# Two of four weight sums added by the vector engine in the second half's Strassen steps, and the down projection's first sums fetched one by one

## The chip, the cores and the metric

The kernel runs on one core of a Trainium2 chip. TensorE (PE in the profile) multiplies matrices, VectorE (DVE) and ScalarE (ACT) work element by element, GpSimd (POOL) and SyncE (SP) issue transfers here. Transfers run on sixteen DMA engines that all queues share. The metric is the device time of one execution in microseconds (us); the profile is one execution of its own, with its own time.

## The reference, cut to what matters

One layer of an encoder: a combined input projection, a recurrent group and an attention group, an output projection, and an MLP, for a sequence of 512 positions and a model width of 1024. The change lies in the MLP, whose hidden width is 4096:

```python
x = x + mix @ w_out[l]
h = rms_norm(x, mlp_norm_g[l])
x = x + jnp.square(jax.nn.relu(h @ w_up[l])) @ w_down[l]
return rms_norm(x, final_norm_g)
```

`w_up` is 1024 x 4096 and `w_down` 4096 x 1024, all in float32.

## The kernel before, in words

**Three products for one.** A float32 matrix is split into a high and a low part. `conv_hi` (line 236) rounds a raw weight tile to its high part `whi` on ScalarE, and `conv_lo` (line 244) subtracts that from the raw tile on VectorE and gives the low part `wlo`. `mm3` (lines 273 to 275) then multiplies high by high, one high by the other's low, and the reverse.

**Chunks.** All weights are cut into tiles of 128 x 1024 floats (512 KB), one chunk each, in the list `chunks`. While TensorE works on chunk c, `feed` converts chunk c + 3: the high part after the third, the low part after the fifth of its eight groups of products. There are four buffers each for `whi` and `wlo`. Chunks that come plainly from memory go through three buffers `wraw`; each `conv_lo` of such a chunk ends with `emit_dma` (line 223), which sends for the next plain chunk on SP's queue into the freed buffer.

**The MLP in two halves of 2048 hidden columns.** In each half some groups of four hidden tiles, called quads and named by their first tile f0, are done by Strassen's scheme (in Winograd's form) with seven block products instead of eight; single tiles are done plainly, and one of them stands in the middle of every quad:

```python
QKIND = ("11", "t1", None, "t2", "21", "t3", "22", "t4")
```

`None` is the plain tile. Kinds "11", "21", "22" use a block of the weights as it stands; t1 to t4 are sums of blocks: t1 = 12 + 11, t2 = t1 + 22, t4 = t2 + 21, t3 = 12 + 22. A Strassen step has 24 products of 256 columns, a plain tile 24 of 512. The first half has two quads; the second half runs tile 12, then the quads f0 = 0 with tile 13, f0 = 8 with tile 14, f0 = 4 with tile 15, and then its down projection.

**How a sum is made.** `load_t` fetches block 12 plainly on SP's queue (line 1144) and then lets an adding fetch on POOL's queue (line 1145) add block 11 (t1) or 22 (t3) to the tile in place. When t1's low part has been made, `conv_lo` sends an adding fetch of block 22 onto the same tile (line 250), which makes t2; after t2's low part another one of block 21, which makes t4. Each adding fetch waits on POOL's queue, in order, for the low part that last read the tile. The raw tiles of the sums have four buffers `tw`. `swap` exchanges the places of t2 and 21 in the order of conversion, not of use.

**Around a step.** `quad_evac` (lines 1153 to 1168) copies a step's result from the accumulators on ScalarE or adds it to an earlier one on VectorE, with the squared ReLU. When all four quarters of two hidden pairs are there, `up_pair` (lines 1076 to 1079) forms the sums of the activations for the down projection, and `next_a` splits finished ones into high and low parts (lines 1182 and 1187) in between.

**The down projection** is itself a Strassen scheme over four groups q = 0 to 3: chunks alternate (11, q) and (s1, q), then (s2, q) and (22, q), and so on. Its first sums s1 = 11 + 12 are made by `load_s1`, for each q a plain fetch on SP (line 1246) and an adding fetch on POOL (line 1247) into the tile `ts`, from which s2 and s4 follow by further adding fetches (line 255). In the second half all four are started in the quad f0 = 8:

```python
if half == 1 and unit[1] == 8:
    loads(4, late)
    late["t2", 7] = lambda: load_s1(1, ts)
```

`late[kind, k]` is called after group k of that step; `loads(f0, late)` starts t1's tile of quad f0 at the end of this quad's t1, and t3's at the end of 21.

**Order.** The instructions of TensorE, ScalarE, VectorE and GpSimd stand in the order of this code. SP's transfers are placed by a scheduler, as early as their buffers allow. Every queue works strictly in order.

Of the kernel before, what the change touches and what calls it, by code (L numbers as in the profile page):

```python
# [15 lines left out]
OP = mybir.AluOpType  # L16
# [19 lines left out]
NQ = HF // 4  # L36
# [54 lines left out]
def hybrid_kernel(ctx: ExitStack, tc, xw, xT, w_in, w_v, w_out, w_up, w_dn, gates, vecs, rel, onehot, fg, out):  # L91
    nc = tc.nc
# [21 lines left out]
    def f(t):  # L114
        return t.bitcast(FT)
# [67 lines left out]
    cu, cq, cd_ = {}, {}, []  # L183
# [19 lines left out]
    raws, splits = {}, {}  # L203
    st = {"rc": 0}

    def ublock(h, b, f):
        return w_up[h * HF + f + {"11": 0, "12": 1, "21": 2, "22": 3}[b]]

    def source(c):
        if not isinstance(c, tuple):  # L210
            return c
        return ublock(*c[:3]) if len(c) == 4 else wblock(*c)

    def wblock(h, b, q):
        return w_dn[h, int(b[1]) - 1, (int(b[0]) - 1) * NQ + q]
# [3 lines left out]
    def emit_dma():  # L219
        if plain:  # L220
            i = plain.popleft()
            r = stream.tile([P, 1024], FT, name="wraw", tag="wraw", bufs=3)
            nc.sync.dma_start(r, source(chunks[i]))
            raws[i] = r


    swap = {}
    for (h, f0, kind), i in cq.items():
        if kind in ("t2", "21"):
            swap[i] = cq[h, f0, {"t2": "21", "21": "t2"}[kind]]  # L230

    def conv_hi(i):
        if i < len(chunks):
# [5 lines left out]
    def conv_lo(i):  # L239
        if i < len(chunks):  # L240
            i = swap.get(i, i)
            r = raws.pop(i)
            lo = stream.tile([P, 1024], FR, name="wlo", tag="wlo", bufs=4)
            nc.vector.tensor_tensor(lo, r, f(splits[i][0]), op=OP.subtract)  # L244
            splits[i] += (lo,)
            c = chunks[i]
            if isinstance(c, tuple) and c[1][0] == "t":
                nxt = {"t1": ("t2", "22"), "t2": ("t4", "21")}.get(c[1])
                if nxt:
                    nc.gpsimd.dma_start(r, ublock(c[0], nxt[1], c[2]), accum_op=OP.add)  # L250
                    raws[cq[c[0], c[2], nxt[0]]] = r
            elif isinstance(c, tuple) and c[1][0] == "s":
                nxt = {"s1": ("s2", "22"), "s2": ("s4", "21")}.get(c[1])
                if nxt:
                    nc.gpsimd.dma_start(r, wblock(c[0], nxt[1], c[2]), accum_op=OP.add)
                    raws[cd_[c[0]] + {"s2": 2 * NQ + 2 * c[2], "s4": 6 * NQ + c[2]}[nxt[0]]] = r
            else:
                emit_dma()

    def feed(c, k):  # L260
        if k == 2:
            conv_hi(c + 3)
        elif k == 4:
            conv_lo(c + 3)

    def feed_q(c, k):
        if k == 1:
            conv_hi(c + 3)
        elif k == 5:
            conv_lo(c + 3)  # L270
# [331 lines left out]
    for i in (3, 4, 5):  # L602
        conv_lo(i)
# [43 lines left out]
    for n, (k, tt) in enumerate(steps):  # L647
        c = C_V + k // 2
# [12 lines left out]
        if n >= GA and n < GA + 12 and (n - GA) % 3:  # L661
            t, m = (n - GA) // 3, 2 * ((n - GA) % 3 - 1)
# [320 lines left out]
    c = C_WO + 4  # L983
# [158 lines left out]
    def load_t(half, n, f0):  # L1142
        t = work.tile([P, 1024], FT, name="tw", tag="tw", bufs=4)
        nc.sync.dma_start(t, ublock(half, "12", f0))
        nc.gpsimd.dma_start(t, ublock(half, {"t1": "11", "t3": "22"}[n], f0), accum_op=OP.add)
        raws[cq[half, f0, n]] = t

    def quad_evac(kind, f0, bank, keep):
# [91 lines left out]
        xf[tt] = g_("xf")  # L1240
        nc.vector.tensor_tensor(xf[tt], x1n[tt, 1], fgt[1], op=OP.mult)

    def load_s1(half, ts):
        for q in range(NQ):
            t = ts[:, q, :]
            nc.sync.dma_start(t, wblock(half, "11", q))
            nc.gpsimd.dma_start(t, wblock(half, "12", q), accum_op=OP.add)
            raws[cd_[half] + 2 * q + 1] = t
# [7 lines left out]
    ts = None  # L1256
    nr2 = {}
    for half in range(2):
# [6 lines left out]
        if half == 0:  # L1265
            start = 3
            load_t(0, "t1", 4)
            pu = [ps_("pu", "pj") for _ in range(start)]
            for k in range(KD):
                for i in range(start):  # L1270
                    mm3(pu[i], wk(c0 + i, k), h2k(k), k == 0, k == KD - 1)
                    if i == 0:
                        feed(c0, k)
                if k in (1, 2, 4, 5):
                    h_sums({1: 0, 2: 1, 4: 2, 5: 3}[k])
                if k == 3:
                    load_t(0, "t3", 4)
                if k == 3:
                    x1_transpose(0, 0)
                if k in (5, 7):  # L1280
                    h_hi("t1", k // 7)
                    h_lo("t1", k // 7)
            conv_hi(c0 + 4)
            conv_lo(c0 + 4)
            for i in (0, 1):
                up_evac(i, pu[i])
            conv_hi(c0 + 5)
            conv_lo(c0 + 5)
            up_evac(2, pu[2])
# [12 lines left out]
        def up_tile(ff, late=()):  # L1302
            p = ps_("pu", "pj")
            c = cu[half, ff]
            for k in range(KD):
                mm3(p, wk(c, k), h2k(k), k == 0, k == KD - 1)
                feed(c, k)
                if (ff, k) in late:
                    late[ff, k]()
                if k in (5, 7):  # L1310
                    next_a()
            up_evac(ff, p)

        def up_quad(f0, mid, late):
            bank, keep = {}, {}
            for kind in QKIND:
                if kind is None:
                    up_tile(mid, late)
                    continue
                x = {"t1": "c", "22": "c", "21": "b"}.get(kind, "a")  # L1320
                if x not in bank:
                    bank[x] = ps_("pu", {"a": "gs", "b": "pj", "c": "et"}[x])
                c = cq[half, f0, kind]
                hi, lo = splits[c]
                for n in range(8):
                    e, k = n // 4, n % 4
                    sl = slice(n * P, (n + 1) * P)
                    mm3(bank[x][:, e * TH:(e + 1) * TH], (hi[:, sl], lo[:, sl]), h_part(kind, k),
                        n == 0 and kind in ("11", "t1", "21"), n == 7, True)
                    feed(c, n)  # L1330
                    if (kind, n) in late:
                        late[kind, n]()
                    if n == 6:
                        next_a()
                quad_evac(kind, f0, bank, keep)

        def split_h(n, m):
            def run():
                h_hi(n, m)
                h_lo(n, m)  # L1340
            return run

        def xt(tt, n):
            return lambda: x1_transpose(tt, n)

        def loads(f0, late):
            late["t1", 7] = lambda: load_t(half, "t1", f0)
            late["21", 7] = lambda: load_t(half, "t3", f0)

        for unit in UNITS[half][start:]:  # L1350
            ready = set(opdone)
            late = {}
            if half == 0 and unit[1] == 4:
                late = {("11", 0): split_h("t2", 0), ("11", 5): split_h("t2", 1), ("t1", 1): split_h("t3", 0), ("t1", 6): split_h("t3", 1),
                        (3, 1): split_h("22", 0), (3, 6): split_h("22", 1),
                        ("t1", 5): xt(0, 1), ("t2", 5): xt(1, 0), ("21", 5): xt(1, 1), ("t3", 5): xt(2, 0), ("22", 5): xt(2, 1), ("t4", 5): xt(3, 0)}
                loads(8, late)
            if half == 0 and unit[1] == 8:
                late = {("11", 5): xt(3, 1), ("t1", 5): scale_neg, (12, 0): lambda: load_s1(0, ts)}
            if half == 1 and unit[1] == 12:  # L1360
                late = {(12, 1): split_h("t1", 0), (12, 5): split_h("t1", 1)}
            if half == 1 and unit[1] == 0:
                late = {("11", 1): split_h("t2", 0), ("11", 5): split_h("t2", 1), ("t1", 1): split_h("t3", 0), ("t1", 5): split_h("t3", 1),
                        (13, 1): split_h("22", 0), (13, 6): split_h("22", 1)}
                loads(8, late)
            if half == 1 and unit[1] == 8:
                loads(4, late)
                late["t2", 7] = lambda: load_s1(1, ts)
            if unit[0] == "q":
                up_quad(unit[1], unit[2], late)  # L1370
            else:
                up_tile(unit[1], late)
# [47 lines left out]
        for j in range(7 * NQ):  # L1420
            _, w, q = seq[j]
# [20 lines left out]
            if half == 0 and j == 25:  # L1442
                h_load()
                ts = big.tile([P, NQ, 1024], FT, name="ts", tag="bigA")
# [82 lines left out]
```

## Time and profile before

| What | Value |
|---|---|
| median of 3 runs | 556.71 us |
| lowest, highest | 556.18, 558.02 us |
| the profiled execution | 556.5 us |
| its span, first to last instruction | 554.7 us |
| granted TensorE clock | 0.998 |
| TensorE, weight load, VectorE, ScalarE, GpSimd busy | 98%, 82%, 76%, 61%, 13% |
| read from memory, written | 94.33 MB, 4.23 MB |

The page of the profile lists busy time by engine, then groups of instructions by line, operation and tile, written output <- inputs. The word after an arrow in a bracket or behind a bar is what ended the idle time before an instruction. Matmuls are pipelined, so their lengths overlap and a busy TensorE need not be at its peak; the distance between starts tells more. In the names, `pu` is an accumulator of the up projection and `pd` of the down projection, `h2h` and `h2l` the parts of the activations, `hh` and `hl` those of their Strassen sums, `whi` and `wlo` the parts of a weight chunk, `wraw`, `tw` and `ts` raw weights, `a` an activation tile, `as` a sum of such, `ah` and `al` parts of one.

### The profile page before, as it was taken

How to read it: one execution, taken by the hardware profiler on the slowest of the kernel's cores; microseconds unless marked ns; L12 is line 12 of the kernel's file. 1: busy time of each engine (PE TensorE's matmuls, PEld its weight loads, DVE VectorE, ACT ScalarE, POOL GpSimd, SP SyncE). 2: the span in 40 equal slices, each digit the busy share in tenths (PEclk: the TensorE clock that was granted, in tenths of full speed). 3: DMA queues.
4: the chain of work that ended last, by engine and by line, in shares of the span. 5: the costliest groups of instructions: out<-in, count | busy, mean ns of one | idle time of the engine just before them, and what ended most of it. 6: DMA issues, size and time to landing. Idle time of an engine off the chain costs nothing. (4 is left out here: it accounts for less than half of the span.)

```text
span 554.7 us, 7754 instructions
## 1 busy us (share of the span) xinstructions
PE 544.7 (98%) x2878; PEld 456.1 (82%) x2878; DVE 421.1 (76%) x614; ACT 335.7 (61%) x531; POOL 71.2 (13%) x93
## 2 busy tenths in 40 slices
PE   9999999999999999999999999999999989999994
PEld 7888888677768668899998888888899979888883
DVE  6897499987677538977659984976664768995894
ACT  7669993688776425577634553754543445655565
POOL 3480000000000010011110114010102200131000
PEclk9999999999999999999999999999999999999999
DMA  7814424454372226387895499997597974799804
GB/s 267 266 39 147 163 92 146 121 164 133 97 266 76 77 77 151 108 234 167 244 240 186 117 262 255 252 334 258 133 302 235 239 194 115 167 314 256 212 0 151
DMA packets 31028, 100.62 MB, mean 181 GB/s; under 512 B 3716, under 2 KB 4100, under 8 KB 30992
## 3 DMA queue, kind: packets, MB, share of 16 engines
q1 hardware_dynamic: 22560, 71.31, 36.6%
q0 software_dynamic: 7680, 27.71, 26.5%
q10 hardware_dynamic: 752, 1.12, 0.6%
q8 instruction: 22, 0.36, 0.3%
q14 instruction: 14, 0.11, 0.1%
HBM read 94.33 MB, written 4.23 MB: 178 GB/s over the span
## 5 line engine op out<-in xcount | busy, mean ns | idle before, releaser
L244 DVE TENSOR_TENSOR wlo<-wraw,whi 128x1024 fp32r<-128x1024 f32 x76 | 93.6, 1234 | 27.1 <-ACT whi L236 27.0
L236 ACT ACTIVATE whi<-wraw 128x1024 fp32r<-128x1024 f32 x76 | 80.3, 1057 | 37.6 <-PE pd L275 13.2
L273 PE MATMUL pd<-whi,ah 128*128 128x512 f32 x192 | 74.8, 390 | 0.1
L274 PE MATMUL pd<-wlo,ah 128*128 128x512 f32 x192 | 74.8, 390 | 0.0
L275 PE MATMUL pd<-whi,al 128*128 128x512 f32 x192 | 74.7, 389 | 0.0
L273 PE MATMUL pu<-h2h,whi 128*128 128x256 f32 (+1 forms) x216 | 71.9, 333 | 0.0
L274 PE MATMUL pu<-h2l,whi 128*128 128x256 f32 (+1 forms) x216 | 71.4, 330 | 0.0
L275 PE MATMUL pu<-h2h,wlo 128*128 128x256 f32 (+1 forms) x216 | 71.3, 330 | 0.0
L244 DVE TENSOR_TENSOR wlo<-tw,whi 128x1024 fp32r<-128x1024 f32 x28 | 34.3, 1223 | 24.1 <-ACT whi L236 24.0
L273 PE MATMUL pu<-hh,whi 128*128 128x256 f32 x160 | 45.7, 286 | 0.7 <-ACT whi L236 0.7
L275 PE MATMUL pu<-hh,wlo 128*128 128x256 f32 x160 | 45.4, 284 | 0.8 <-DVE wlo L244 0.8
L236 ACT ACTIVATE whi<-ts 128x1024 fp32r<-128x1024 f32 x24 | 25.5, 1062 | 32.7 <-PE pd L275 18.4
L274 PE MATMUL pu<-hl,whi 128*128 128x256 f32 x160 | 45.3, 283 | 0.0
L273 PEld LDWEIGHTS pu<-h2h,whi 128*128 128x128 f32 x216 | 41.0, 190 | 3.8 <-ACT x1n L1047 0.2
L275 PEld LDWEIGHTS pu<-h2h,wlo 128*128 128x128 f32 x216 | 41.0, 190 | 3.8
L274 PEld LDWEIGHTS pu<-h2l,whi 128*128 128x128 f32 x216 | 41.1, 190 | 3.6
L236 ACT ACTIVATE whi<-tw 128x1024 fp32r<-128x1024 f32 x28 | 29.5, 1053 | 23.1 <-DMA tw<-in_w_up_dram 13.3
L273 PEld LDWEIGHTS pd<-whi,ah 128*128 128x128 f32 x192 | 36.0, 188 | 8.0 <-issue 0.5
L274 PEld LDWEIGHTS pd<-wlo,ah 128*128 128x128 f32 x192 | 36.0, 188 | 7.6 <-DVE wlo L244 0.2
L275 PEld LDWEIGHTS pd<-whi,al 128*128 128x128 f32 x192 | 36.0, 188 | 7.4
L244 DVE TENSOR_TENSOR wlo<-ts,whi 128x1024 fp32r<-128x1024 f32 x24 | 29.3, 1221 | 16.1 <-ACT whi L236 16.0
L273 PEld LDWEIGHTS pu<-hh,whi 128*128 128x128 f32 x160 | 30.7, 192 | 1.3 <-ACT whi L236 1.2
(247 smaller groups left out, 1252.1 us busy)
## 6 DMA issues: line engine op xcount, KB each, us to landing
wraw<-in_w_up_dram SPq DMA_DIRECT2D x27, 512.0 KB, 4.3
ts<-in_w_dn_dram POOLq DMA_DIRECT2D x24, 512.0 KB, 13.0
wraw<-in_w_dn_dram SPq DMA_DIRECT2D x24, 512.0 KB, 7.9
tw<-in_w_up_dram POOLq DMA_DIRECT2D x20, 512.0 KB, 8.4
wraw<-in_w_in_dram SPq DMA_DIRECT2D x13, 512.0 KB, 3.4
tw<-in_w_up_dram SPq DMA_DIRECT2D x10, 512.0 KB, 9.3
wraw<-in_w_out_dram SPq DMA_DIRECT2D x8, 512.0 KB, 3.3
ts<-in_w_dn_dram SPq DMA_DIRECT2D x8, 512.0 KB, 10.4
```

Source lines behind the costliest of these rows:

```text
L236: act(hi, raws[i], AF.Copy)
L244: nc.vector.tensor_tensor(lo, r, f(splits[i][0]), op=OP.subtract)
L273: nc.tensor.matmul(o, lhsT=a[0], rhs=b[0], start=bool(first), stop=False, skip_group_check=on)
L274: nc.tensor.matmul(o, lhsT=a[0], rhs=b[1], start=False, stop=False, skip_group_check=on)
L275: nc.tensor.matmul(o, lhsT=a[1], rhs=b[0], start=False, stop=bool(last), skip_group_check=on)
```

## The change

Only the second half's quads change (`half` or `c[0]` equal to 1). The order of conversion in them becomes 11, t1, plain tile, 21, 22, t2, t3, t4; the order of use stays. 22's raw tile is added by VectorE onto t3's tile, which then holds block 12 alone, right after 22's low part is made; the adding fetch of 22 for t3 goes. 21's raw tile is held in its buffer, and after t2's low part VectorE adds it onto that tile, which makes t4; the adding fetch of 21 goes. The next plain fetch is sent after the add, so for 21 it is sent when t2 has been converted and not when 21 has. In the first half the new table gives the same order as before.

The down projection's first sums of the second half are started singly: q = 0 after the last group of t3 in the quad f0 = 8, and q = 1, 2, 3 in the quad f0 = 4, after the first group of 11, the first of t1 and the fifth of t2.

```diff
-    swap = {}
+    SPLIT = (("11", "t1", None, "21", "t2", "t3", "22", "t4"), ("11", "t1", None, "21", "22", "t2", "t3", "t4"))
+    swap, held = {}, {}
     for (h, f0, kind), i in cq.items():
-        if kind in ("t2", "21"):
-            swap[i] = cq[h, f0, {"t2": "21", "21": "t2"}[kind]]
+        if kind == "11":
+            for j in range(8):
+                if SPLIT[h][j] is not None:
+                    swap[i + j] = cq[h, f0, SPLIT[h][j]]
...
                 if nxt:
-                    nc.gpsimd.dma_start(r, ublock(c[0], nxt[1], c[2]), accum_op=OP.add)
+                    if c[0] == 1 and c[1] == "t2":
+                        nc.vector.tensor_tensor(r, r, held.pop("21"), op=OP.add)
+                        emit_dma()
+                    else:
+                        nc.gpsimd.dma_start(r, ublock(c[0], nxt[1], c[2]), accum_op=OP.add)
                     raws[cq[c[0], c[2], nxt[0]]] = r
+            elif isinstance(c, tuple) and len(c) == 4 and c[0] == 1 and c[1] == "21":
+                held["21"] = r
+            elif isinstance(c, tuple) and len(c) == 4 and c[0] == 1 and c[1] == "22":
+                t = raws[cq[c[0], c[2], "t3"]]
+                nc.vector.tensor_tensor(t, t, r, op=OP.add)
+                emit_dma()
...
         nc.sync.dma_start(t, ublock(half, "12", f0))
-        nc.gpsimd.dma_start(t, ublock(half, {"t1": "11", "t3": "22"}[n], f0), accum_op=OP.add)
+        if half == 0 or n == "t1":
+            nc.gpsimd.dma_start(t, ublock(half, {"t1": "11", "t3": "22"}[n], f0), accum_op=OP.add)
...
-    def load_s1(half, ts):
-        for q in range(NQ):
+    def load_s1(half, ts, qs=range(NQ)):
+        for q in qs:
...
             if half == 1 and unit[1] == 8:
                 loads(4, late)
-                late["t2", 7] = lambda: load_s1(1, ts)
+                late["t3", 7] = lambda: load_s1(1, ts, (0,))
+            if half == 1 and unit[1] == 4:
+                late = {(("11", 0), ("t1", 0), ("t2", 4))[q - 1]: lambda q=q: load_s1(1, ts, (q,)) for q in range(1, NQ)}
```

## The prediction

> **What bounds the kernel now.** I read the page's busy shares first, then busy time by stretches of the second half, then TensorE's instructions in order of time where a stretch is not full, then the chain that ends there, and last the queues that feed that chain.
>
> ```profile
> span 554.7 us, 7754 instructions
> PE 544.7 (98%) x2878; PEld 456.1 (82%) x2878; DVE 421.1 (76%) x614; ACT 335.7 (61%) x531; POOL 71.2 (13%) x93
> ...
> q1 hardware_dynamic: 22560, 71.31, 36.6%
> q0 software_dynamic: 7680, 27.71, 26.5%
> ```
>
> The second half of the MLP runs from 386.8 us. In the next fence the columns are the stretch, its length, and the busy time of each engine in it; the second stretch is the only one in which TensorE is not full before the end.
>
> ```profile
> core 0: us, PE busy (x) PEld busy (x) DVE busy (x) ACT busy (x) POOL busy (x), PEclk, DMA share, GB/s
> 386.80:454.40 67.60, 67.60 (x480) 63.87 (x479) 44.01 (x53) 29.34 (x41) 11.59 (x13) 1.00 0.87 232
> 454.40:457.10 2.70, 1.21 (x6) 0.58 (x6) 1.53 (x2) 2.62 (x4) 0.01 (x1) 1.00 0.04 15
> 471.20:547.90 76.70, 76.45 (x338) 62.76 (x336) 64.48 (x86) 47.91 (x72) 9.75 (x11) 1.00 0.70 185
> ```
>
> So a change that touches only feeding can win what lies in that one hole, and little more. The hole in TensorE's order of time (start, length, engine, line, operation):
>
> ```profile
> 454.23 0.39 PE L274 MATMUL pu<-h2l,whi 128*128 128x512 f32 x1
> 454.46 0.39 PE L275 MATMUL pu<-h2h,wlo 128*128 128x512 f32 x1
> 455.59 0.39 PE L273 MATMUL pu<-hh,whi 128*128 128x256 f32 x1 [0.74 <-ACT whi L236]
> 455.81 0.28 PE L274 MATMUL pu<-hl,whi 128*128 128x256 f32 x1
> 456.85 0.39 PE L275 MATMUL pu<-hh,wlo 128*128 128x256 f32 x1 [0.76 <-DVE wlo L244]
> 457.07 0.28 PE L273 MATMUL pu<-hh,whi 128*128 128x256 f32 x1
> 457.19 0.28 PE L274 MATMUL pu<-hl,whi 128*128 128x256 f32 x1
> ```
>
> Lengths overlap, so I count starts. A 512-column product starts 0.23 us after the one before it, a 256-column one 0.12. After 454.46 the next should start at 454.69 and starts at 455.59 (0.90 lost); then 0.22 for 0.12 (0.10), 1.04 for 0.12 (0.92), and 0.22 for 0.12 (0.10). The sum is **2.02 us**. It is the first product of step t2 in the last quad (f0 = 4), first its high and then its low weight part. The chain behind it (start, length, what):
>
> ```profile
> 440.75 13.65 DMA tw<-in_w_up_dram
> ...
> 454.48 1.07 ACT whi L236
> ```
>
> The DMA is the adding fetch that turns t1's tile into t2's, sent from POOL. Why it took 13.65 us shows on POOL's issues, and in what that line usually takes (least, median, most of ten):
>
> ```profile
> 426.08 0.88 POOL L250 DMA_DIRECT2D tw<-in_w_up_dram  x1 [10.07 <-DVE wlo L244]
> 426.62 1.23 POOL L1145 DMA_DIRECT2D tw<-in_w_up_dram  x1
> 427.17 4.29 POOL L1247 DMA_DIRECT2D ts<-in_w_dn_dram  x4
> 429.36 3.00 POOL L1145 DMA_DIRECT2D tw<-in_w_up_dram  x1
> 440.75 0.88 POOL L250 DMA_DIRECT2D tw<-in_w_up_dram  x1 [8.39 <-DVE wlo L244]
> ```
>
> ```profile
> DMA to landing us min/median/max: 5.2/5.5/13.6
> ```
>
> Seven adding fetches go out within 3.3 us, four of them the down projection's first sums. By the page's queue lines, 27.71 MB in pieces of 512 KB are 53 adding fetches, and 26.5% of 554.7 us shared among them is 2.8 us each on all sixteen engines; a plain fetch comes to 1.5 the same way. Seven at 2.8 are 20 us of work, to 446 without any plain fetch between them, so t2's, sent at 440.75, stands behind the last of them.
>
> **The change, part by part.**
>
> *Two adding fetches per quad go (t3's 22, t4's 21), in three quads.* Six times 2.8 is 17 us of DMA time out of the first stretch, where the DMA share is 0.87 of 67.6, or 59 us. TensorE is full there, so this is worth nothing by itself; it is a cause of the next item.
>
> *The four sums of the down projection are spread.* In the built program, POOL now has q0's sum behind t1's of the last quad, then t2's adding fetch (sent by the same low-part conversion as now, near 440.75), and only then q1, q2, q3. POOL does not follow TensorE: nothing but their landed first halves holds q1 to q3, so they go out directly behind t2's, which is ahead of them in the same queue. SP's plain fetches of those first halves stand early in SP's order (the first waits only for the reads of the saved activations), so POOL should not stand waiting for them. With the queue empty, t2's fetch should take the median, 5.5 us, and land at 446.3; at the 8.6 that a queue of a few would give, at 449.4. Its high part takes 1.07 us, so any landing before 453.5 is hidden. The DMA wait falls from 2.02 us to **0**. Below nothing it can't go, since TensorE has no other idle time there.
>
> *What is late next: DVE.* Conversions went 11, t1, tile, 21, t2, t3, 22, t4; they go 11, t1, tile, 21, 22, t2, t3, t4. t2's low part is one place later, and ahead of it stand 22's low part and the new add t3 += 22. DVE around the last quad:
>
> ```profile
> 440.78 0.69 DVE L1164 TENSOR_TENSOR a<-v,pu 128x512 f32<-128x512 f32 x1 [0.33 <-PE pu L275]
> ...
> 448.44 0.69 DVE L1079 SCALAR_TENSOR_TENSOR as<-as,a 128x512 f32<-128x512 f32 x1
> 449.04 1.22 DVE L244 TENSOR_TENSOR wlo<-wraw,whi 128x1024 fp32r<-128x1024 f32 x1
> 450.18 0.68 DVE L1187 TENSOR_TENSOR al<-a,ah 128x512 fp32r<-128x512 f32 x1
> 455.57 1.23 DVE L244 TENSOR_TENSOR wlo<-tw,whi 128x1024 fp32r<-128x1024 f32 x1 [4.71 <-ACT whi L236]
> ```
>
> From 440.78, released by TensorE, to 450.18 DVE has no idle time: evacuation and the pair sums of two finished pairs. Then it waits 4.71 us for t2's high part. Now that hole is filled. Back to back, a 1024-column operation holds DVE 1.14 us (449.04 to 450.18) and a 512-column one 0.60 (448.44 to 449.04). The new order from 449.04 is low part of 21, a split of 512, low part of 22, the add, a split, low part of t2: it starts at 449.04 + 1.14 + 0.60 + 1.14 + 1.14 + 0.60 = 453.66 and ends 1.23 later, at 454.89. TensorE wants it for the third product, at 454.69 + 0.24 = 454.93, and started 0.05 after the end in the profile (455.57 + 1.23 to 456.85). That is 0.01 late, so DVE is exactly on the edge. No row shows the add itself. The nearest two-input operations (mean length in ns after the bar):
>
> ```profile
> L244 DVE TENSOR_TENSOR wlo<-wraw,whi 128x1024 fp32r<-128x1024 f32 x12 | 14.6, 1221 | 4.2 <-ACT whi L236 4.2
> L1376 DVE SCALAR_TENSOR_TENSOR x1n<-pd,r,x1n 128x512 f32<-128x512 f32 x2 | 1.4, 744 | 0.0
> ```
>
> I take the first, the same width with both inputs in the same memory as here. The lower end is a t2 part in time, 0 lost. For the upper end I let every operation hold DVE for its full length: 1.22 + 0.68 + 1.22 + 1.22 + 0.68 + 1.23 = 6.25, ending at 455.29, 0.41 late, with 0.10 for the restart as above 0.5. An add like the second row, twice 0.744 or 1.49, makes it 0.8. I take **0.1**, since the spacing of starts is what these very operations show.
>
> Behind t2's low part stand the second add (t2 += 21), two splits, the tile's two squares and t3's low part: 454.80 + 1.14 + 4 x 0.60 + 1.23 = 459.6, wanted at 454.69 + 2 steps of 2.88 + 0.24 = 460.7. t3's and t4's high parts on ACT now wait for these adds (ready near 453.1 and 456.0) instead of adding fetches, ahead of the evacuations on ACT, and are wanted later than that; cost **0**, with 1.1 us to spare.
>
> *The other two quads.* A quad is seven steps of 24 products at 0.12 and a tile of 24 at 0.227, together 25.6 us, so t2's steps of the three quads start near 403.5, 429.1 and 454.7. DVE in the first one (f0 = 0):
>
> ```profile
> 394.58 1.23 DVE L244 TENSOR_TENSOR wlo<-wraw,whi 128x1024 fp32r<-128x1024 f32 x1 [0.25 <-ACT whi L236]
> 395.72 1.42 DVE L1133 TENSOR_TENSOR hl<-hs,hh 128x512 fp32r<-128x512 f32 x2
> 397.40 1.23 DVE L244 TENSOR_TENSOR wlo<-tw,whi 128x1024 fp32r<-128x1024 f32 x1 [0.26 <-ACT whi L236]
> 398.54 1.48 DVE L1133 TENSOR_TENSOR hl<-hs,hh 128x512 fp32r<-128x512 f32 x2
> ```
>
> At 397.40 would stand 22's low part, the add to 399.7, the two activation splits to 401.2, t2's low part to 402.5, wanted after 403.7: cost **0**. The second quad has neither splits nor pair sums there, so more.
>
> *Plain stream.* 21's block keeps one of three raw buffers until t2's low part is made, so the blocks behind it on SP are sent a tile later; they are wanted five and more steps on. 22's block is sent as now, but converted one step and one tile, 8.3 us, earlier. The tightest is that of the second quad, sent at 412 and so long on its way (line, size, us to landing; stretch 411.9 to 412.1):
>
> ```profile
> wraw<-in_w_up_dram SPq DMA_DIRECT2D x1, 512.0 KB, 11.7
> ```
>
> After its landing follow its high part (1.07), its low part and the add (1.14 each) and t2's low part (1.23), 4.6 us, in that order on ACT and DVE; t2's is wanted at 429.3. So it may land as late as 424.7, 12.7 us after it was sent; 11.7 would do, and that stretch loses two adding fetches. Cost **0**, by a cover of 1 us; without it, us for us.
>
> *The late sums.* q1 to q3 land at 2.8 us each behind 446.3, by 455; the first conversion that reads one of them comes after the last quad, near 469. Cost **0**.
>
> *Sum.* 2.02 - 0.1 = 1.9 us, with ends 1.2 (slow add) and 2.0. Against the profiled execution: 556.5 - 1.9 = 554.6. Its span is 554.7, with 1.8 around it; the median of the runs is 556.71, 0.2 above, so I give **554.8 us**, which is 0.34% less. What a measurement of this kernel can tell from no change is about 0.3%, or 1.7 us, so the forecast lies just past the edge.
>
> **Rivals.**
>
> *DVE takes part of it back.* Place: t2's low part in the last quad. Every 0.1 us that DVE is behind the row of starts above costs 0.1. With operations that never overlap, 0.5 is lost and the time is 556.7 - 1.5 = 555.2; with slow adds 555.5. For it: DVE has no slack left from 440.78 on. Against: starts 1.14 apart for 1.22 long. [...]
>
> *The gain is given back in the down projection, or t2 stays late.* ACT waited there once for a sum:
>
> ```profile
> ACT whi L236 <- DMA ts<-in_w_dn_dram: 6.0, 1, 6.0
> ```
>
> If the fetches there go at their own pace, TensorE comes 2 us earlier and waits 2 us: 556.7. Against: they are sent when buffers come free, so they move with TensorE, and TensorE is busy 76.45 of 76.70 us. The same time comes out if q0's sum holds POOL and t2's fetch is sent as late as 449.
>
> *Slower: the raw stream starves.* 22's fetch in the second quad takes longer than 12.7 us. Each us beyond is lost to TensorE; from 14.6 on the loss passes the gain of 1.9, and at 18 us 5.3 are lost and the time is 560.1. For it: 11.7 was seen, and there ACT's wait would hold everything behind it. Against: the fetch stood behind plain fetches of all four first halves, which SP's new order partly puts after it, and behind two adding fetches that are gone (5.6 us).
>
> **How the numbers follow.** Forecast 0.60; DVE takes part 0.16; given back 0.12; slower 0.12. The forecast's own spread, 554.2 to 555.2, crosses 555.04 (0.3%), so a little of it counts as no change: faster 0.53, same 0.35, slower 0.12. Range: from 554.0 (hole gone, and the 0.25 us of the down projection with part of the 0.2 between runs) to 557.2 (given back, with 0.5 for the spread of runs), leaving out the slower case.
>
> **What would show it.** Right: t2's adding fetch in the last quad 5 to 9 us long; three sums behind it; six new operations of 1.2 us on DVE; the step from the last tile's product to t2's first 0.23 us, and the low part at most 0.3 late; seven adding fetches from the line that is L250 now, and seven from L1145, instead of ten each. Wrong: ACT waiting for a raw block in the second quad past 424.7; a hole of TensorE in another quad or in the down projection; an add well over 1.3 us.

## The result, and the profile after

The changed kernel takes 553.73 us (median of 6 runs, 553.33 to 554.95); the kernel before, on the same chip, takes 556.68 (6 runs). The ratio is 0.9948, with a 95% interval from 0.9933 to 0.9963: faster, by 2.1 to 3.7 us. Forecast were 554.8 us and a range from 554.0 up; the time lies 0.27 us below that range. The profiled execution took 553.66 us. (Of two experiments below, e8 and e12, the profiled execution was disturbed; their traces are not read and their times leave it out.) The head of the page after:

```profile
span 551.9 us, 7746 instructions
PE 543.2 (98%) x2878; PEld 455.7 (83%) x2878; DVE 428.2 (78%) x620; ACT 336.0 (61%) x531; POOL 66.2 (12%) x87
...
q1 hardware_dynamic: 22560, 71.31, 37.0%
q0 software_dynamic: 6816, 24.57, 23.9%
```

Six adding fetches of 512 KB (27.71 - 24.57 = 3.14 MB) have gone from the software queue, and DVE has six operations more, for 7.1 us more. TensorE's work is the same. Busy time by stretches, the same ones as before, moved to where they now lie:

```profile
core 0: us, PE busy (x) PEld busy (x) DVE busy (x) ACT busy (x) POOL busy (x), PEclk, DMA share, GB/s
386.10:453.60 67.50, 67.50 (x480) 63.74 (x479) 51.99 (x61) 33.41 (x47) 8.03 (x9) 1.00 0.73 193
453.60:456.30 2.70, 2.70 (x22) 2.58 (x21) 2.67 (x4) 1.61 (x3) 0.00 (x0) 1.00 0.66 220
468.50:545.10 76.60, 76.35 (x338) 62.90 (x336) 63.37 (x84) 47.97 (x72) 9.78 (x11) 1.00 0.70 184
```

The stretch that had TensorE busy for 1.21 of 2.70 us is full. In the first one DVE rises from 44.01 to 51.99 us, and the DMA share falls from 0.87 to 0.73. TensorE in order of time, at the last quad's t2:

```profile
453.79 0.39 PE L288 MATMUL pu<-h2h,wlo 128*128 128x512 f32 x1
454.02 0.28 PE L286 MATMUL pu<-hh,whi 128*128 128x256 f32 x1
454.13 0.28 PE L287 MATMUL pu<-hl,whi 128*128 128x256 f32 x1
454.25 0.39 PE L288 MATMUL pu<-hh,wlo 128*128 128x256 f32 x1
454.47 0.28 PE L286 MATMUL pu<-hh,whi 128*128 128x256 f32 x1
```

t2's first product comes 0.23 us after the plain tile's last one, and the low part's product at its place; only the start behind that is 0.22 later instead of 0.12. Of the 2.02 us, 0.10 is left. The reason stands on POOL's queue (line 257 is the adding fetch of line 250 before, line 1261 that of 1247) and, in the second fence, in the landing times of all fetches of line 257:

```profile
440.07 0.87 POOL L257 DMA_DIRECT2D tw<-in_w_up_dram  x1 [22.94 <-DVE wlo L247]
440.62 3.03 POOL L1261 DMA_DIRECT2D ts<-in_w_dn_dram  x3
```

```profile
DMA to landing us min/median/max: 5.3/5.4/7.8
```

t2's fetch goes out at the old time, ahead of three of the sums, and takes 5.4 us instead of 13.65. POOL worked in order there: the first halves of those sums had been sent by 412.2 and took 7.5 us at most (line 1260), and the sums still went out behind t2's fetch, for which POOL waited 22.94 us. DVE there:

```profile
448.37 1.22 DVE L247 TENSOR_TENSOR wlo<-wraw,whi 128x1024 fp32r<-128x1024 f32 x1
449.50 0.69 DVE L1201 TENSOR_TENSOR al<-a,ah 128x512 fp32r<-128x512 f32 x1
450.10 1.22 DVE L247 TENSOR_TENSOR wlo<-wraw,whi 128x1024 fp32r<-128x1024 f32 x1
451.24 1.22 DVE L263 TENSOR_TENSOR tw<-tw,wraw 128x1024 f32<-128x1024 f32 x1
452.38 0.69 DVE L1201 TENSOR_TENSOR tw<-as,tw 128x512 fp32r<-128x512 f32 x1
452.98 1.22 DVE L247 TENSOR_TENSOR wlo<-tw,whi 128x1024 fp32r<-128x1024 f32 x1
454.23 1.23 DVE L254 TENSOR_TENSOR tw<-tw,wraw 128x1024 f32<-128x1024 f32 x1
```

This is the worked-out order, operation by operation, with no idle time in it. The low part ends at 454.20 and its product starts at 454.25.

By the starts of the first products of each stage (us; the last two columns are the second half):

| kernel, execution | second half starts | up projection | down projection |
|---|---|---|---|
| before, profiled | 386.79 | 84.37 | 76.10 |
| after, profiled | 386.12 | 82.38 | 75.96 |

The up projection lost 1.99 us, the down projection 0.14. The remaining 0.67 of the 2.82 us between the spans lies ahead of the second half: 0.32 ahead of the MLP and 0.35 in the first half's down projection (76.51 us before, 76.16 after). Up to there the two programs differ in one transfer alone: the adding fetch for t3 of the first quad, which goes out at 368.59 in the kernel before, is gone.

### The profile page after: what moved, and what is told of

The parts are those of the page before. It is cut to its first block, busy times and chain, and to the rows that moved or that the text cites. A ratio compares the mean times of both kernels' runs of the same rounds, so it can differ in the third digit from the quotient of the medians.

```text
span 551.9 us, 7746 instructions
## 1 busy us (share of the span) xinstructions
PE 543.2 (98%) x2878; PEld 455.7 (83%) x2878; DVE 428.2 (78%) x620; ACT 336.0 (61%) x531; POOL 66.2 (12%) x87
## 3 DMA queue, kind: packets, MB, share of 16 engines
q0 software_dynamic: 6816, 24.57, 23.9%
## 4 chain that ended last, share of the span: by engine, by line
PE 94%; DVE 2%; ACT 1%; DMA 1%; issue 0%; SPq 0%; ACTq 0%; DVEq 0%
PE pu L286 10%; PE pu L288 10%; PE pu L287 10%; PE pd L288 8%; PE pd L286 8%; PE pd L287 8%; PE pqk L286 3%; PE pwo L286 3%; PE pwo L288 3%; PE pqk L288 3%; PE pwo L287 3%; PE pqk L287 3%; PE pav L819 3%; PE pt L786 3%; PE pv L288 1%; PE pv L286 1%
## 5 line engine op out<-in xcount | busy, mean ns | idle before, releaser
L287 PEld LDWEIGHTS pu<-hl,whi 128*128 128x128 f32 x160 | 30.7, 192 | 0.2
```

The lines of the kernel that those rows point to most:

```text
L287: nc.tensor.matmul(o, lhsT=a[0], rhs=b[1], start=False, stop=False, skip_group_check=on)
```

## The experiments

Ratios are to the kernel before, run on the same chip beside each group.

**Chance and cause: both kernels once more, and each part of the change alone.** e1 is the kernel before and e2 the changed one, unchanged. e3 has only the sums spread (`load_s1` takes its new argument as in the change, here and in e6):

```diff
-                late["t2", 7] = lambda: load_s1(1, ts)
+                late["t3", 7] = lambda: load_s1(1, ts, (0,))
+            if half == 1 and unit[1] == 4:
+                late = {(("11", 0), ("t1", 0), ("t2", 4))[q - 1]: lambda q=q: load_s1(1, ts, (q,)) for q in range(1, NQ)}
```

e4 is the changed kernel with these lines put back, so that it has only the two adds on DVE.

> The kernel before, unchanged. The changed kernel gained 2.95 us by the medians and 2.8 by the two profiled spans, where the hole in front of t2 explains 2.0. In the profiles, 0.7 us of the rest lies ahead of the change: 0.3 in the first 30 us and 0.35 in the first half's down projection, where both programs are the same. Theory: that 0.7 is chance of single executions, and the hole itself differs between executions. Then the start of the second half (386.8 in the profile before, 386.1 after) falls anywhere from 386.0 to 387.5 here, and the hole anywhere from 1.5 to 3.5 us. Rival: the changed program's first part is really faster; then the second half starts at 386.8 +- 0.1 again, and the hole is 2.0 +- 0.1.

> The changed kernel, unchanged. Theory (chance ahead of the change): the second half starts between 386.0 and 387.5, the two after it (up projection and down projection) take 82.3 and 76.0 us as in the first profile, and the ratio to before is 0.995 to 0.997. Rival (the first part is really faster): the second half starts at 386.1 +- 0.1 again, and the ratio is 0.995 or less.

> The kernel before with the down projection's first sums started one by one as in the change; the adding fetches for t3 and t4 and the old order of conversion stay. Theory: the queue on POOL is all that made t2 late, and four sums were most of it; without them ahead t2's fetch takes 5 to 9 us instead of 13.6, its low part is made at once since the old order puts it before 22's, and the up projection takes 82.3 us as in the changed kernel: the whole gain, 2.0 us in the second half, ratio 0.995 to 0.997. Rival: the six adding fetches that went are needed too, because the queue is full without the sums; then t2 still lands past 453 and at least 0.7 us of the hole stays.

> The changed kernel with all four first sums started where they were before, after t2 in the quad f0 = 8; VectorE's adds and the new order stay. Theory: with two adding fetches per quad gone, the six that go out together from about 414 are worked off by 435, t2's fetch finds the queue empty and takes 5 to 6 us, and this part alone also gives the whole 2.0 us, ratio 0.995 to 0.997. So each part would do alone what both do together. Rival: the sums still hold up t2; then its fetch takes over 9 us and part of the hole is back.

| run | median us | ratio (95%) | second half starts | up | down |
|---|---|---|---|---|---|
| e1, before | 556.09 | 1.0002 (0.9989 to 1.0014) | 385.90 | 84.26 | 76.43 |
| e2, after | 553.57 | 0.9956 (0.9941 to 0.9970) | 385.79 | 82.39 | 75.96 |
| e3, sums spread | 554.09 | 0.9959 (0.9946 to 0.9973) | 385.56 | 82.29 | 75.97 |
| e4, adds only | 553.78 | 0.9954 (0.9940 to 0.9968) | 385.31 | 82.39 | 75.96 |

No gain shows in the first part of the kernel: e1 starts its second half 0.9 us earlier than the profiled execution of the same program. Both starts, 385.90 and 385.79, lie a little below the 386.0 that was the least expected. By the starts e1 loses 1.96 us at its hole, against 2.02. And either half of the change gives the whole gain. The adding fetches of line 250 (257 in e4) landed after (least, median, most) in e3 and in e4:

```profile
DMA to landing us min/median/max: 5.2/5.4/8.4
```

```profile
DMA to landing us min/median/max: 5.1/5.3/8.5
```

t2's own took 5.3 us in both. In e3 it overtakes the sums; in e4 they go out together as before, but the queue has fewer fetches and they have landed by 438.7, before t2's is sent. e3 has no hole at all, e4 the 0.10 that DVE leaves.

**How much one fetch ahead costs.** e6 is the kernel before with the last sum alone moved behind t2's fetch; e7 is the kernel before with 512 KB more of adding fetches behind the four sums, onto tiles that nothing reads.

```diff
-                late["t2", 7] = lambda: load_s1(1, ts)
+                late["t2", 7] = lambda: load_s1(1, ts, (0, 1, 2))
+            if half == 1 and unit[1] == 4:
+                late = {("t2", 4): lambda: load_s1(1, ts, (3,))}
```

```diff
-                late["t2", 7] = lambda: load_s1(1, ts)
+                def more():
+                    load_s1(1, ts)
+                    for i in range(2):
+                        t = g_("extra")
+                        nc.vector.memset(t, 0.0)
+                        nc.gpsimd.dma_start(t, w_dn[0, 0, 0, :, i * S:(i + 1) * S], accum_op=OP.add)
+                late["t2", 7] = more
```

> The kernel before, with three of the four sums of the down projection left where they are and only the last one sent behind t2's adding fetch of the last quad. Theory of the queue (each adding fetch ahead costs t2's about 3 us): t2's fetch lands 2.8 to 3.4 us earlier, near 451 us where up to 453.5 is hidden, so the hole of 2.0 us goes whole, the up projection of the second half takes 82.3 us, ratio 0.995 to 0.997. Rival, the gain goes by the number of sums moved: a quarter of it, 0.5 us, ratio 0.999, up projection 83.9.

> The kernel before, with 512 KB more of adding fetches (two of 256 KB onto tiles that nothing reads) sent directly behind the four sums, ahead of t2's of the last quad. Theory of the queue: t2's fetch lands 2.8 to 3.4 us later, the hole grows from 2.0 to 4.8 to 5.4 us, the kernel is about 3 us slower, ratio 1.005 to 1.006. Rival, the fetch was long for another reason (its own source rows, the plain fetches beside it): under 1 us more, ratio under 1.002.

e6 took 554.02 us, ratio 0.9963 (0.9950 to 0.9977); e7 560.76, ratio 1.0087 (1.0066 to 1.0107). t2's fetch in e6 (its issue, its landing time):

```profile
440.52 0.88 POOL L250 DMA_DIRECT2D tw<-in_w_up_dram  x1 [9.01 <-DVE wlo L244]
```

```profile
DMA to landing us min/median/max: 10.3/10.3/10.3
```

10.3 us instead of 13.65: 3.4 earlier for one fetch fewer, and this hides it whole (up projection 82.29). The chain in e7, and TensorE at the hole:

```profile
439.64 17.16 DMA tw<-in_w_up_dram
...
456.88 1.06 ACT whi L236
```

```profile
453.35 0.39 PE L275 MATMUL pu<-h2h,wlo 128*128 128x512 f32 x1
457.99 0.58 PE L273 MATMUL pu<-hh,whi 128*128 128x256 f32 x1 [4.25 <-ACT whi L236]
458.37 0.41 PE L274 MATMUL pu<-hl,whi 128*128 128x256 f32 x1
459.25 0.58 PE L275 MATMUL pu<-hh,wlo 128*128 128x256 f32 x1 [0.46 <-DVE wlo L244]
```

17.2 us: 3.5 more for one fetch more. So the length of t2's fetch went with the number of fetches ahead, by 3.4 and 3.5 us for one, and with one fewer TensorE saw nothing of it. The expected 3 us of time were too few, though: the up projection takes 89.35, 5.0 us more. The first starts behind the hole stand 0.38 us apart instead of 0.12; the clock, below, is why.

**Is DVE on the edge?** e5 is the changed kernel with t2's low part in the last quad computed three times over, e12 with it computed twice (the repeats change no value):

```diff
             lo = stream.tile([P, 1024], FR, name="wlo", tag="wlo", bufs=4)
+            if chunks[i] == (1, "t2", 4, "u"):
+                for _ in range(2):
+                    nc.vector.tensor_tensor(lo, r, f(splits[i][0]), op=OP.subtract)
             nc.vector.tensor_tensor(lo, r, f(splits[i][0]), op=OP.subtract)
```

> The changed kernel, with the low part of t2 in the last quad computed three times over instead of once (the two extra operations change no value). Theory that DVE stands exactly on the edge there: the finished low part comes 2 x 1.14 = 2.3 us later, TensorE waits 2.3 to 2.4 us ahead of its third product of t2 instead of 0.10, the up projection of the second half goes from 82.4 to 84.7 us, and the kernel is 2.3 us slower than the changed one, ratio to before 0.999 to 1.000. Rival, DVE has slack there or hands the delay on to work that nobody waits for: under 0.5 us more, ratio 0.995. Second question: if the small holes in the down projection of the second half (0.4 us before, none after) come from what a hole in the up projection leaves behind, they come back here and that stage takes 76.2 to 76.5 us; if the adding fetches caused them, it stays at 75.96.

> The changed kernel, with the low part of t2 in the last quad computed twice instead of once. Theory, DVE on the edge and the clock falling only after long holes: a hole of 1.14 + 0.10 = 1.24 us and no lower clock behind it, up projection 83.5 to 83.6 us, 1.14 to 1.3 us above the changed kernel, ratio to before 0.997 to 0.998, no run with a mean clock below 0.996. Rival, any hole lowers the clock: products 0.21 us apart for some 3 us behind it, 2.5 us above the changed kernel.

e12 took 554.99 us, ratio 0.9977 (0.9965 to 0.9989), 1.3 to 1.4 us above the changed kernel (553.57 in e2, 553.73), close to what no slack at all gives; its hole isn't shown. e5 took 557.63, ratio 1.0021 (1.0005 to 1.0036): slower than expected by more than a microsecond. DVE in e5:

```profile
453.06 2.48 DVE L249 TENSOR_TENSOR wlo<-tw,whi 128x1024 fp32r<-128x1024 f32 x2
455.57 1.23 DVE L250 TENSOR_TENSOR wlo<-tw,whi 128x1024 fp32r<-128x1024 f32 x1
456.83 1.23 DVE L257 TENSOR_TENSOR tw<-tw,wraw 128x1024 f32<-128x1024 f32 x1
```

The low part ends at 456.80, 2.60 us after that of the changed kernel; the repeats write one tile and start 1.25 apart, not 1.14. TensorE:

```profile
454.21 0.28 PE L290 MATMUL pu<-hl,whi 128*128 128x256 f32 x1
456.86 0.39 PE L291 MATMUL pu<-hh,wlo 128*128 128x256 f32 x1 [2.36 <-DVE wlo L250]
...
457.56 0.28 PE L290 MATMUL pu<-hl,whi 128*128 128x256 f32 x1
457.68 0.38 PE L291 MATMUL pu<-hh,wlo 128*128 128x256 f32 x1
457.85 0.41 PE L289 MATMUL pu<-hh,whi 128*128 128x256 f32 x1
458.06 0.41 PE L290 MATMUL pu<-hl,whi 128*128 128x256 f32 x1
```

The hole is 2.65 less the usual 0.12, or 2.53 us, as it should be. But 0.9 us behind it the starts go from 0.12 to 0.21 apart. The granted clock in stretches (the third number from the end):

```profile
core 0: us, PE busy (x) PEld busy (x) DVE busy (x) ACT busy (x) POOL busy (x), PEclk, DMA share, GB/s
456.60:457.80 1.20, 0.94 (x7) 0.95 (x8) 1.17 (x2) 0.00 (x0) 0.00 (x0) 0.97 0.00 0
457.80:460.90 3.10, 3.10 (x17) 3.10 (x16) 3.10 (x6) 0.00 (x0) 0.00 (x0) 0.50 0.56 166
460.90:463.00 2.10, 2.10 (x18) 2.10 (x18) 0.84 (x2) 1.54 (x2) 0.00 (x0) 0.95 0.01 4
```

After this hole of 2.53 us TensorE runs at a granted clock of 0.50 for the 3.10 us of the second stretch and for parts of its neighbours (0.97 and 0.95). Some 16 products that take 0.093 us more each are 1.5 us, which is most of the 1.7 us that e5 is later than expected (557.63 less 553.6 is 4.0, where 2.3 were worked out); the rest is the hole itself, 2.53 instead of 2.3. The second question of e5 got its answer too: its down projection takes 75.96 us, so the small holes there (0.08 us in the profiled execution before, 0.37 in e1) don't come from a hole in the up projection.

**Does the order on DVE alone decide?** e8 is e5 with t2 converted ahead of 22; e9 is the same kernel again, for its trace.

```diff
-    SPLIT = (("11", "t1", None, "21", "t2", "t3", "22", "t4"), ("11", "t1", None, "21", "22", "t2", "t3", "t4"))
+    SPLIT = (("11", "t1", None, "21", "t2", "t3", "22", "t4"), ("11", "t1", None, "21", "t2", "22", "t3", "t4"))
```

> As the run with the low part computed three times over, but with t2 converted ahead of 22 in the second half, so that 22's low part and the add t3 += 22 (together 2.28 us of DVE) stand behind t2's low part instead of ahead of it. Theory that only the order on DVE sets the end there: the extra 2.28 us are covered at t2 (hole there 0.1 as in the changed kernel), and t3's low part, which had about 1.0 us to spare, comes 2.28 us later, so TensorE waits 1.0 to 1.3 us at t3; up projection 83.4 to 83.7 us, time between the changed kernel and the run with the low part three times over, ratio about 0.997 to 0.998. Rival, t3 has more spare than worked out: no hole, ratio 0.995. Rival, something beside DVE holds t2: 2.3 us lost again, ratio 0.999 to 1.000.

> The run with t2 converted ahead of 22 once more, for its trace: its 555.3 to 555.6 us are 1.8 us above the changed kernel. Theory that only the order on DVE moved the wait: at t2 0.1 us are lost, at t3 1.0 to 1.3 us, two steps later, and the up projection takes 83.4 to 83.7 us; what is over of the 1.8 us then lies elsewhere. Rival: t2 waits still.

e8 took 555.34 us, ratio 0.9987 (0.9976 to 0.9999), e9 555.47, ratio 0.9994 (0.9978 to 1.0010); 0.997 to 0.998 were expected. In e9 nothing is lost at t2, and this two steps on:

```profile
459.90 0.27 PE L290 MATMUL pu<-hl,whi 128*128 128x256 f32 x1
461.57 0.39 PE L291 MATMUL pu<-hh,wlo 128*128 128x256 f32 x1 [1.41 <-DVE wlo L250]
461.80 0.28 PE L289 MATMUL pu<-hh,whi 128*128 128x256 f32 x1
```

With 0.10 for the restart 1.65 us are lost at t3's low part, where 1.0 to 1.3 were expected; the up projection takes 83.94 us. So the wait moved from t2 to t3 with the order, and of the 2.5 us that the two repeats take, t3 had about 1.0 to spare (2.5 less the 1.56 without a product). Behind this hole of 1.56 us the starts stay 0.12 apart.

**Does the hole of the kernel before lower the clock too?** e10 is the kernel before, unchanged. e11 is the kernel before with twelve products of zeros in the hole, so that TensorE idles less while t2's weights come no sooner:

```diff
+                if (half, f0, kind) == (1, 4, "t1"):
+                    zero[0] = g_("zero", FR)[:, :TH]
+                    nc.vector.tensor_scalar(zero[0], h2h[:, 0, left], 0.0, None, op0=OP.mult)
+                if (half, f0, kind) == (1, 4, "t2"):
+                    for n in range(12):
+                        nc.tensor.matmul(bank[x][:, 0:TH], lhsT=h2h[:, n % 8, left][:, 0:P], rhs=zero[0], start=False, stop=False, skip_group_check=True)
                 for n in range(8):
```

> The kernel before, unchanged, for the granted clock. With the low part computed three times over, the hole of 2.5 us at t2 was followed by 3.1 us at a granted clock of 0.50, which cost 1.4 us more than the hole. New theory: the hole of 2.02 us of the kernel before sets this off too, but only in some executions, since it is cut in two; those have a mean clock of 0.994 to 0.995 and a span near 555.2 us, the others 0.996 to 0.998 and near 554.0. Expected: about a quarter of the runs of the first kind, ten or more us apart from nothing else; if the profiled one is of it, the products behind t2's hole stand 0.21 us apart instead of 0.12 for about 3 us. Rival, the low mean clock comes from the start of the kernel, which varies by 1.2 us: then runs without the hole show it as often.

> The kernel before, with twelve products of a tile of zeros (256 columns, 0.12 us each, 1.44 us in all) added ahead of t2's first product in the last quad; they add nothing to the sums. t2's weights come no sooner, so the end of the hole stays where it is (low part at about 456.8), but TensorE idles there for 0.5 to 0.7 us instead of 2.02. Theory that idle time in the hole lowers the clock in some executions: no run has a mean clock of 0.995 or less, and the median is 0.2 to 0.4 us below that of before, ratio 0.9993 to 0.9996, near 554.0 us of span. Rival, the clock has nothing to do with the hole: as many low clocks as before, ratio 1.000; if the products delay t2 instead, 0.1 to 0.5 us more.

e10 took 556.46 us, ratio 1.0007 (0.9991 to 1.0022). Its profiled execution was one of those with a low mean clock (0.995, span 556.3). In stretches:

```profile
core 0: us, PE busy (x) PEld busy (x) DVE busy (x) ACT busy (x) POOL busy (x), PEclk, DMA share, GB/s
458.20:458.40 0.20, 0.20 (x4) 0.20 (x4) 0.20 (x1) 0.20 (x2) 0.11 (x1) 1.00 0.00 0
458.40:458.60 0.20, 0.20 (x4) 0.20 (x3) 0.20 (x1) 0.20 (x1) 0.00 (x0) 0.77 0.00 0
458.60:461.00 2.40, 2.40 (x13) 2.40 (x12) 2.40 (x5) 1.77 (x4) 0.00 (x0) 0.50 0.86 125
...
461.80:462.00 0.20, 0.20 (x3) 0.20 (x2) 0.20 (x1) 0.07 (x1) 0.00 (x0) 0.70 1.05 205
462.00:462.20 0.20, 0.20 (x4) 0.20 (x3) 0.20 (x1) 0.00 (x0) 0.00 (x0) 1.00 0.22 41
```

Its hole was the usual one (by the starts, 0.94 + 0.10 + 0.92 + 0.10 = 2.06 us), and 1.3 us after the low part's product at 457.20 the clock goes to half, from about 458.5 to 461.9, by the shares of the stretches at 0.77 and 0.70. The up projection takes 85.84 us, 1.5 more than in the other two profiles of this kernel. That is the direct sight of it; the runs give how often. In e7 the clock falls inside the hole, at 455.91 (0.80 over 453.30:457.70, then 0.50 to 462.60), and is back only 6.83 us later, which is where its time beyond the hole went. A mean clock of 0.995 or less over the whole execution (the hole is the time without a product by the starts, without the 0.10 behind each piece):

| kernels | hole, us | runs with it |
|---|---|---|
| before (in all groups with a clock for each run) | 1.8 in two pieces | 21 of 95 |
| after, e2, e3, e4, e6 | none | 1 of 30 |
| e12 | 1.25 (worked out) | 0 of 9 |
| e8, e9 | 1.56 | 0 of 17 |
| e5 | 2.53 | 8 of 10 |
| e7 | 4.4 and 0.8 | 4 of 4 |

Of the 95, those 21 have a mean span of 555.42 us, the others 554.20, so 1.2 us each. The start of the kernel can't be the reason: the kernels without the hole start in the same way, and only one of their 30 runs has the low clock, with a span (552.2) no longer than the others'.

e11 took 556.36 us, ratio 1.0005 (0.9993 to 1.0017). None of its 12 runs has the low clock, which at 21 in 95 has a chance of 5%. Its median isn't lower, though, as expected by 0.2 to 0.4 us; the interval reaches from 0.4 us of gain to 0.9 of loss, so this side is not settled. The products cost a little themselves: they end too late for t2's first product, and its low part comes 0.1 us later than in the profiled execution before (up projection 84.45):

```profile
454.26 1.59 PE L1332 MATMUL pu<-zero,h2h 128*128 128x256 f32 x12
455.69 0.28 PE L273 MATMUL pu<-hh,whi 128*128 128x256 f32 x1
455.81 0.28 PE L274 MATMUL pu<-hl,whi 128*128 128x256 f32 x1
456.55 0.39 PE L275 MATMUL pu<-hh,wlo 128*128 128x256 f32 x1 [0.46 <-DVE wlo L244]
```

## Why the prediction was right, and where it was wrong

**The hole and its cause: right.** t2's fetch stood behind other adding fetches, and was expected to take 5.5 us with the queue empty; it took 5.4. The price of 2.8 us for each fetch ahead was low: e6 and e7 measure 3.4 and 3.5 on either side. It changed nothing: the 10.3 us of e6 already left no hole, and t2's fetch took 5.4.

**DVE on the edge: right.** The worked sum said 0.01 late and 0.1 lost; 0.10 was lost. The add that no row of before showed took 1.22 us, the row it was taken from, and starts stand 1.14 apart. With that the rival in which operations don't overlap, with 555.2 us, falls: the rows from 450.10 to 452.38 start 1.14 us apart for 1.22 of length. Where an operation writes the tile that the one before it reads or writes, the rows here show no early start: in e5 the repeats start 1.25 us apart for 1.23 of length, and the add behind t2's low part starts 1.25 after it (452.98 to 454.23). e12 and e5 show the edge from the other side: each operation more ahead of t2's low part is paid in full. The 1.1 us to spare at t3 held: in the changed kernel its low part is done at 459.00 and its product starts at 460.10, and in e9 2.5 us of delay left TensorE 1.56 without a product.

**The other costs of nothing: right.** No hole appeared in another quad. 22's block of the second quad, for whose landing I had about 1 us of cover, kept nobody waiting: ACT converted it at 420.74 straight after the evacuation before it. The down projection took nothing back, since 75.96 us is the least of all traces. So the given-back and the slower rival fall too. The 17 us of DMA time taken out of the first stretch were too many: of the six adding fetches one went out ahead of it (368.59) and one behind it (457.1), and its DMA share fell from 0.87 of 67.6 to 0.73 of 67.5, or by 9.5 us. TensorE was full there, so nothing hung on it.

**The sum's base, and the low end of the range: wrong.** The step was "against the profiled execution: 556.5 - 1.9 = 554.6", with 0.2 to the median of the runs, and the end of 554.0 that allowed the 0.25 us of the down projection and part of 0.2 between runs. Against all runs the 554.8 were 1.1 us too high. The base is 0.6 of this: 556.71 was the median of three runs, and that of the 95 runs of the kernel before in the table above is 556.10. The gain is the other 0.5: down to 553.69, the median of twelve runs of the changed kernel, it is 2.4 us, where 1.9 were forecast. Three things were mis-sized.

First, the spread from one execution to the next in the shared part. The second half started at 386.79 in the profiled execution, and between 385.56 and 387.10 in the seven traces of kernels that are the same up to there (385.31 to 386.20 in the five with one adding fetch fewer). That alone can be the 0.67 of the 2.82 us between the two profiles. I took 0.2 from two times that happened to lie close together.

Second, the clock. I priced the hole as the time in which TensorE stood still. In e10 the clock halves behind it, and 21 of 95 executions have the low mean clock that goes with this. The mean span of the 95 is 554.47 us, of those at the high clock 554.20: so 0.27 us of the mean go with the clock. The profiled execution was not of this kind (0.998), and so couldn't show it.

Third, the down projection of the second half. The 0.25 us that I counted as its idle time, 76.45 of 76.70, is there after the change as well, 76.35 of 76.60, and was no gain to be had. Small holes that only starts show were: 0.08 us in the profiled execution and 0.37 in e1, where the stage is 0.14 and 0.47 longer than 75.96, and none in e10. Their cause is open; e5 only excludes the hole.

Over all these runs the mean span goes from 554.47 (95) to 552.12 (30 runs of kernels without the hole): 2.35 us, of which 1.9 to 2.0 are the hole, 0.27 the clock, and the rest, about 0.1, fits the down projection. So the 2.95 us between the first two medians are the upper part of what chance allows, and the change itself is worth about 2.35. The interval of e2, 1.7 to 3.3 us, agrees.

No version here beats the changed kernel by what can be measured. e3 shows that spreading the sums is enough, without the adds; what is left in the up projection is 0.10 us.

## What to carry to other kernels

A transfer that is wanted soon should not stand behind a burst of transfers that are wanted late, when their queue works in order, as POOL's did: here each one ahead cost 3.4 to 3.5 us, and moving a single one was enough, since 3.4 us less hid the whole hole of 2.02. Price a hole in TensorE with what may follow it (here 3.41 us at half clock in e5 and e10), and look for that in the granted clock of many runs, because one profile may be of an execution that was spared. And when a forecast is made against one execution, take its spread from the parts that the change doesn't touch, over as many traces as there are.

## What the runs showed of the hardware that was not expected

TensorE's granted clock fell to half behind holes of about 2 us, in some executions. Behind 2.53 us without a product it fell in 8 of 10 runs, behind 1.8 us in two main pieces in 21 of 95, behind 1.56 us in none of 17, by the mean clock of each run. It fell 0.9 (e5) and 1.3 us (e10) after the low part's product, and by the shares of the stretches it came back 3.41 us later in both, while TensorE was busy all the time: 457.72 to 461.13 in e5 (0.79 in 457.60:457.80, 0.68 in 461.00:461.20) and 458.51 to 461.92 in e10.

The traces show the same hole with and without this:

| execution | without a product, us | clock behind it | up projection |
|---|---|---|---|
| e10 | 0.94 and 0.92 | half | 85.84 |
| before, profiled | 0.90 and 0.92 | full | 84.37 |
| e1 | 1.74 in all | full | 84.26 |

What makes the difference between these three executions is not shown.
